# One hybrid decoder layer on one core: the 64-row products of two heads issued in turn, an own PSUM bank for the outputs of the recurrence, and two pieces of setup placed behind other work

## The chip, the core and the metric

The kernel runs on one core of one Trainium2 chip. The time of a run is that of one execution on the device, in microseconds (us). Before the change three runs gave 782.29, 787.22 and 790.95 us; the median is 787.22.

The engines in the profile are PE (TensorE's products), PEld (its weight loads), DVE (VectorE), ACT (ScalarE), POOL (GpSimd) and SP (SyncE, which issues the DMAs). A label such as L359 is a line of the kernel before; in the changed kernel the same statements stand some lines lower.

## What is computed

One decoder layer on 1024 tokens of width 1024, all in float32. A normed input is projected once; one part feeds four heads of latent attention, one part eight heads (64 wide) of a recurrence, and one part gates both.

```python
u = rmsnorm(h, norm_pre_g);  p = u @ w_in
p_mla, p_rw, z = split(p)
q, kv = ...                                  # low-rank; rope on 64 columns of q and of the key
y_mla = causal softmax attention of 4 heads  # 128 + 64 wide scores
r, k, v, xw, xa = token_shift_mix(p_rw)
decay = exp(-exp(-softplus(-(w0 + tanh(xw) @ w2)) - 0.5));  a = sigmoid(a0 + xa @ a2)
# recurrence, for each head and token:
S = S * w_t + (S @ -kk_t) (kk_t * a_t)^T + v_t k_t^T;   y_t = S @ r_t
y_rw = group_norm(y) * g + b + bonus
h = h + rmsnorm((concat(y_mla, y_rw) * silu(z)) @ w_out, norm_post_g)
```

## The kernel before

Tokens are done in two halves of 512, h = 0 and 1; inside a half the recurrence runs over 8 chunks of 64 tokens. Channels of the recurrence are four blocks of 128, and a block holds two heads: head e = 0 on partitions 0 to 63, e = 1 on 64 to 127. Two blocks make a group g, so a half has two groups of four heads.

A string `PROGRAM` lists the steps in the order in which they are recorded; a step is a letter and its indices. The whole lies in a block with a scheduler, which then places the instructions on each engine by its own model of time, so an engine's order is not that of the string: steps overlap, and products of later steps stand between those of earlier ones. Each engine then runs its list in order. Tiles with the same tag share a fixed number of buffers: in PSUM four of `pj` (projections), two of `wk`, two of `ch`, each of one bank. In SBUF `LS`, `BK`, `AB` and `SV` have two buffers each, one for each group, so the second half's units (and later the attention's tiles, which use the same tags) take them when the first half is done with them.

The steps that matter here:

- **A** (stage_a): for each of four blocks of 128 tokens of the half, the sum of squares (ACT), on POOL the two operations of `rstd` (L57, L58), on DVE the scaling (L170), on PE eight transposes (L177), and the split of the result into a high and a low part `uH` (ACT, L181) and `uL` (DVE, L182). All projections (L210) read both parts.
- **X** (op_x, lora_in): in half 0 first the low-rank weights, loaded and split on POOL (L232, L233, two of each); then one projection, shifted (L218), tanh, and the parts `xw` and `xa` that the products L250 and L251 read. Weights of a projection are split by ACT (L190) and POOL (L200, four pieces each).
- **B** (op_b): tables of sine and cosine for the rope: 25 operations on DVE (L655 to L676; L661 eight times, L667 four times) and two Sin on ACT. They are read only by the attention's steps.
- **P** (prep): projections and elementwise work for one block of 128 channels.
- **E** (units): for that block the products inside the chunks. L359: for each chunk and head a 64-row product `(64 x 128)^T (64 x 128)` into `pE[e]`, one `wk` bank for a head and four chunks; DVE reads each twice (L363, L364). L373: for each chunk and head a 64-row product with 64 columns into `pB`, one `wk` bank for a head and eight chunks, read by DVE (L374). L384 is a 128-row product and L392 four more. The masked triangles go to DRAM for the inverse.
- **I** (inverse): 62 operations on DVE (L418, L420) invert all 32 x 32 triangles, the result comes back by DMA (`sx`, `st`), then 32-row products (L447, L454) and copies into `AB` (L455, L456) finish the 64 x 64 inverses.
- **C** (chain): chunk after chunk, for both groups: R from the state (L474), copied by ACT (L476); part of the output Y (L480); the corrected values (L484), copied by ACT and DVE (L486, L487); the new state (L490), added by DVE (L494); the rest of Y (L496), copied by ACT (L499). All four results of a group lie in one `ch` bank, `pcs`:

```python
pcs = [chp((128, 4, 2, 64)) for _ in range(2)]   # 0: R, 1: Y, 2: corrected, 3: state
PE.matmul(pc[ev[e], 3, l], BK[:, l, c, e], SV[:, c, e, l], ...)      # L490
V.tensor_tensor(dst, pc[ev[e], 3], D_[ev[e]], ALU.add)               # L494
PE.matmul(pc[ev[e], 1, l], AB[ev[e], l, c, 64:128], SV[...], ...)    # L496
S.copy(SV[:, c, 0], pc[:, 1])                                        # L499
```

- **N, G**: group norm (L513) and outputs, whose transposes L525 take one head at a time, 64 rows, into a `ch` bank. **M, T**: the attention's projections (L538 to L540, 96 products a half) and their tail (L563). **Z, Y**: the gates (L210; L586 for two gates at once). **U, K, J, Q, S**: the attention and the output projection (L728, L758, L774, L794, L801, L819, L842, L863, L874, L922); some of their PSUM tiles are `wk` buffers too.

Of the kernel before, what the change touches and what calls it, by code (L numbers as in the profile page):

```python
# [44 lines left out]
def layer(tc, x, pos, w_in, w_out, w_uq, w_ukv, vecs, w2, a2, consts, post_g, out):  # L45
# [9 lines left out]
    def rstd(ss, scale):  # L55

        G.tensor_scalar(ss, ss, scale, EPS, ALU.mult, ALU.add)  # L57
        G.tensor_tensor(ss, ss, mhalf[:, 0:ss.shape[-1]], ALU.pow)  # L58
# [4 lines left out]
    with tc.tile_pool(name="sb", bufs=1) as cp, \  # L63
# [58 lines left out]
        ops.update(attention(tc, E))  # L122
        for op in " ".join(PROGRAM).split():
            name = op.rstrip("0123456789")
            ops[name](*(int(i) for i in op[len(name):]))
# [4 lines left out]
    "A0 X0 Z00 B P00 E00 Z01 P01 E01 Z02 P02 E02 P03 E03 I0 C0 N00 G00 N01 G01 M0 Z03 Z04 Z05 Y06 T0 A1 X1",  # L130
    "P10 E10 Z10 P11 E11 Z11 P12 E12 P13 E13 I1 C1 N10 G10 N11 G11 M1 Z12 T1 Z13 Z14 Z15 Z16 Z17 U K J Q0",
    "Q1 Q2 Q3 S",
)


def recurrence(tc, E):
# [13 lines left out]

    uH = alloc(P1, (128, 8, HALF), "uH", F32R)
    uL = alloc(P1, (128, 8, HALF), "uL", F32R)

    def stage_a(h):

        XT = (("v", "sq"), ("sg", "cs"), ("a", "k"), ("kf", "r"))
        for pr in range(2):
            xs = []
            for q in range(2):
# [8 lines left out]
                E["rstd"](ss[:, 0:1], 1.0 / D)  # L168
# [66 lines left out]
    def lora_in(h):  # L235
        px = shifted(proj(CO_X), V_MU_X, "v", 1)
# [8 lines left out]
        return xw, xa  # L245
# [100 lines left out]
    def units(h, cb, gt, made):  # L346
# [6 lines left out]
        for c4 in range(0, NCH, 4):  # L353
            mk = mks[c4 // 4]
            pE = [wk((128, 4, 128)) for _ in range(2)]
            for ci in range(4):
                for e in range(2):
                    r = slice(e * 64, e * 64 + 64)
                    PE.matmul(pE[e][:, ci], pl[r, c4 + ci, 1 - e:3 - e].rearrange("p a b -> p (a b)"),  # L359
                              LS[r, c4 + ci, e, :], start=True, stop=True)  # L360
# [7 lines left out]
        G.tensor_tensor(dD, bc(id2.unsqueeze(1), (128, NCH, 64)), bc(Dg.unsqueeze(2), (128, NCH, 64)), ALU.mult)  # L368
        for e in range(2):
            r = slice(e * 64, e * 64 + 64)  # L370
            pB = wk((128, NCH, 64))
            for c in range(NCH):
                PE.matmul(pB[:, c], pl[r, c, 1 - e:3 - e].rearrange("p a b -> p (a b)"), dD[r, c], start=True, stop=True)  # L373
            V.tensor_tensor(BK[:, :, e], pB, bc(rs[:, :, e:e + 1], (128, NCH, 64)), ALU.mult)  # L374
# [22 lines left out]

    ev = (slice(0, 64), slice(64, 128))
    le = [(l, e) for l in range(2) for e in range(2)]

    def inverse(h, gt):
# [37 lines left out]
        for g in range(2):  # L439
# [9 lines left out]
            for l in range(2):  # L449
# [5 lines left out]
                V.tensor_copy(AB[0:32, l, :, 32:64], pG[0:32])  # L455
                S.copy(AB[64:96, l, :, 32:64], pG[64:96])  # L456

    def chain(h, gt):

        for g in range(2):  # L460
            for e in range(2):
                G.tensor_copy(gt["g"][g]["SV"][ev[e], 0, e], Sst[ev[e], 2 * g:2 * g + 2])
        for c in range(NCH):
# [4 lines left out]
            parts = []  # L468
            for g in range(2):
                LS, BK, AB, SV = (gt["g"][g][k] for k in ("LS", "BK", "AB", "SV"))  # L470
                parts.append((LS, BK, AB, SV, Sst[:, 2 * g:2 * g + 2], gt["Dg"][:, 2 * g:2 * g + 2], pcs[g], Rs[g], SD[g]))
            for LS, BK, AB, SV, St, Dg, pc, R_, D_ in parts:
# [4 lines left out]
                for e in range(2):  # L477
                    G.tensor_tensor(D_[ev[e]], SV[ev[e], c, e], bc(Dg[ev[e], :, c:c + 1], (64, 2, 64)), ALU.mult)  # L478
                for l, e in le:
                    PE.matmul(pc[ev[e], 1, l], LS[:, l, c, e, 64:128], SV[:, c, e, l], start=False, stop=False,  # L480
                              skip_group_check=True)
            for LS, BK, AB, SV, St, Dg, pc, R_, D_ in parts:
                for l, e in le:
                    PE.matmul(pc[ev[e], 2, l], AB[ev[e], l, c, 0:64], R_[ev[e], l], start=False, stop=False,  # L484
                              skip_group_check=True)
                S.copy(SV[ev[0], c, 0], pc[ev[0], 2])  # L486
# [574 lines left out]
```

## Time and profile before

| what | before |
|---|---|
| runs: lowest, median, highest | 782.29, 787.22, 790.95 us |
| the profiled execution | 783.81 us |
| its span in the trace | 782.0 us |
| mean granted clock of TensorE | 0.951 of full |
| busy: PE, PEld, DVE, ACT, POOL | 713.0, 586.1, 466.4, 347.9, 331.9 us |
| idle TensorE: L177 waiting for its last input from DRAM at the start | 9.8 us |
| idle TensorE: L490 waiting for L487 | 4.9 us in 9 |
| idle TensorE: L177 waiting for L170 | 3.4 us in 1 |

In a row of a timeline stand the start, the duration, engine, line, operation, output and inputs, and in brackets the idle time before it with what ended it. A row may hold several instructions (`x8`); its duration then runs from the first start to the last end. A float32 product appears as two instructions. Products are pipelined: an instruction's duration is longer than the distance to the next start, so the pace is read from start to start. In the tables by stretch of time the columns are the stretch, its length, busy time and instructions of each engine, the granted clock, the share of the DMA engines and GB/s.

### The profile page before, as it was taken

To read this page: it belongs to the slowest core of one execution; us is meant where nothing else is said; L and a number is where in the kernel's file an instruction comes from. 1 tells how busy PE (TensorE), PEld (TensorE's weight loads), DVE (VectorE), ACT (ScalarE), POOL (GpSimd) and SP (SyncE) were. 2 spreads that over 40 slices of the span, in tenths; PEclk is the share of its full clock that TensorE was granted. 3 is DMA by queue.
4 is the path that set the end of the run, shared out by engine and by line. 5 is a ranking of instruction groups with operands and counts; after the bars stand their busy time and mean duration, and the time that the engine had idled before them with its cause. 6 is when DMAs were issued, how large, how long until landed. Compare 5 with 4: busy or idle time off the path is not lost. (4 is left out here: it accounts for less than half of the span.)

```text
span 782.0 us, 13855 instructions
## 1 busy us (share of the span) xinstructions
PE 713.0 (91%) x5136; PEld 586.1 (75%) x5136; DVE 466.4 (60%) x943; ACT 347.9 (44%) x877; POOL 331.9 (42%) x478
## 2 busy tenths in 40 slices
PE   2789999999978998889999989799899998899996
PEld 1667877789866776667888967577678997788885
DVE  4756757758925522495866691476497767644333
ACT  6465355343725453344353162426354566632221
POOL 6265645445942554263554374032332237442220
PEclk9999999999998899977999989879999999999999
DMA  6224241254383133043223366411023025144321
GB/s 208 80 69 115 54 114 51 68 151 134 114 187 89 28 108 83 2 89 85 57 68 97 86 171 156 131 44 42 2 55 101 21 89 162 52 166 141 121 82 54
DMA packets 118819, 72.84 MB, mean 93 GB/s; under 512 B 47072, under 2 KB 108256, under 8 KB 118752
## 3 DMA queue, kind: packets, MB, share of 16 engines
q1 hardware_dynamic: 118752, 71.96, 32.5%
q8 instruction: 40, 0.66, 0.4%
q14 instruction: 27, 0.22, 0.1%
HBM read 54.38 MB, written 17.56 MB: 92 GB/s over the span
## 5 line engine op out<-in xcount | busy, mean ns | idle before, releaser
L210 PE MATMUL pj<-uH,w 128*128 128x512 f32 x640 | 215.7, 411 | 3.3 <-DVE uL L182 2.5
L200 POOL TENSOR_TENSOR w<-wf,w 128x256 fp32r<-128x256 f32 x168 | 141.3, 871 | 116.6 <-ACT w L190 106.5
L210 PEld LDWEIGHTS pj<-uH,w 128*128 128x128 f32 x640 | 123.7, 195 | 33.1 <-DVE uL L182 2.9
L210 PE MATMUL pj<-uL,w 128*128 128x512 f32 x320 | 130.2, 407 | 0.0
L210 PEld LDWEIGHTS pj<-uL,w 128*128 128x128 f32 x320 | 62.6, 196 | 14.0 <-issue 0.8
L190 ACT CAST w<-wf 128x1024 fp32r<-128x1024 f32 (+1 forms) x50 | 51.4, 1027 | 28.8 <-PE pj L540 21.3
L478 POOL TENSOR_TENSOR SD<-SV,Dg 64x128 f32<-64x128 f32 x64 | 27.9, 436 | 74.0 <-DVE SV L494 59.9
L854 POOL TENSOR_SCALAR wf<-wf,sm 128x128 f32<-128x128 f32 (+7 forms) x32 | 24.0, 750 | 67.1 <-DVE sm L853 51.9
L198 POOL TENSOR_TENSOR w<-wf,w 128x224 fp32r<-128x224 f32 x32 | 23.8, 775 | 38.8 <-ACT w L190 32.2
L359 PEld LDWEIGHTS wk<-LS,pl 64*128 64x128 f32 x256 | 30.2, 191 | 12.5 <-issue 10.2
L979 DVE TENSOR_TENSOR LS<-pj,LS 128x512 f32<-128x512 f32 x16 | 11.1, 691 | 45.5 <-ACT cq L978 44.3
L359 PE MATMUL wk<-LS,pl 64*128 64x128 f32 x256 | 35.6, 289 | 1.3 <-DVE LS L317 1.2
L850 ACT ACTIVATE wf<-pj,mx 128x512 f32<-128x512 f32 (+3 forms) x48 | 27.7, 583 | 13.5 <-DVE mx L847 9.9
L865 ACT CAST BK<-wk 128x512 fp32r<-128x512 f32 (+3 forms) x48 | 22.4, 485 | 25.2 <-PE wk L863 23.2
L373 PEld LDWEIGHTS wk<-r,pl 64*128 64x128 f32 x256 | 29.5, 196 | 4.4 <-issue 2.9
L373 PE MATMUL wk<-r,pl 64*128 64x64 f32 x256 | 31.2, 284 | 1.2 <-DVE LS L364 1.0
L874 PE MATMUL ch<-BK,LS 128*128 128x256 f32 (+1 forms) x160 | 31.6, 282 | 0.7 <-ACT BK L865 0.7
L487 DVE COPY SV<-ch 64x128 f32<-64x128 f32 x32 | 9.2, 294 | 36.5 <-issue 25.7
L418 DVE TENSOR_TENSOR tmp<-XA 128x31 f32<-128x31 f32 (+15 forms) x62 | 28.2, 454 | 4.4 <-DMA XA<-sa 2.6
L866 DVE TENSOR_TENSOR AB<-wk,BK 128x512 fp32r<-128x512 f32 (+3 forms) x48 | 26.0, 551 | 7.3 <-ACT BK L865 6.8
L420 DVE TENSOR_TENSOR XA<-XA,tmp 128x31 f32<-128x31 f32 (+15 forms) x62 | 28.4, 458 | 1.9
L845 DVE TENSOR_REDUCE mx<-pj 128x1 f32<-128x512 f32 (+3 forms) x48 | 25.8, 551 | 6.0 <-PE pj L844 3.4
(339 smaller groups left out, 1659.4 us busy)
## 6 DMA issues: line engine op xcount, KB each, us to landing
wf<-in_w_in_dram SPq DMA_DIRECT2D x42, 512.0 KB, 3.9
zs<-st SPq DMA_DIRECT2D x16, 256.0 KB, 3.1
wf<-in_x_dram SPq DMA_DIRECT2D x8, 512.0 KB, 3.7
out_dram<-LS SPq DMA_DIRECT2D x16, 256.0 KB, 2.1
wf<-in_w_in_dram SPq DMA_DIRECT2D x8, 448.0 KB, 3.5
bvd<-st SPq DMA_DIRECT2D x8, 256.0 KB, 2.0
SV<-bvd SPq DMA_DIRECT2D x16, 128.0 KB, 3.4
yrw<-SV SPq DMA_DIRECT2D x8, 256.0 KB, 2.6
```

Of the source, the lines that this page charges most:

```text
L190: S.copy(wh, wf)
L200: G.tensor_tensor(wl[:, sl], wf[:, sl], wh[:, sl].bitcast(F32), ALU.subtract)
L210: PE.matmul(ps, w_[:, kb], u_[:, kb], start=(n == 0), stop=(n == 23))
L359: PE.matmul(pE[e][:, ci], pl[r, c4 + ci, 1 - e:3 - e].rearrange("p a b -> p (a b)"), LS[r, c4 + ci, e, :], start=True, stop=True)
L373: PE.matmul(pB[:, c], pl[r, c, 1 - e:3 - e].rearrange("p a b -> p (a b)"), dD[r, c], start=True, stop=True)
L418: V.tensor_tensor(t3, bc(At[:, j, j + 1:32].unsqueeze(2), (128, n, w)), bc(X[:, j, 0:w].unsqueeze(1), (128, n, w)), ALU.mult)
L420: V.tensor_tensor(X[:, j + 1:32, 0:w], X[:, j + 1:32, 0:w], t3, ALU.add)
L478: G.tensor_tensor(D_[ev[e]], SV[ev[e], c, e], bc(Dg[ev[e], :, c:c + 1], (64, 2, 64)), ALU.mult)
L845: V.tensor_reduce(mx[:, n5:n5 + 1], s_, axis=AX.X, op=ALU.min)
L850: S.activation(pr[:, b0:b1], sc[:, 0:b1 - b0], AF.Exp, bias=mx[:, 0:1], scale=-1.0, accum_out=sm[:, n5:n5 + 1])
L866: V.tensor_tensor(PL[:, b0:b0 + nb, o], pt[:, 0:nb], PH[:, b0:b0 + nb, o].bitcast(F32), ALU.subtract)
L874: PE.matmul(py[:, o], l_, r_, start=(j == 0 and n == 0), stop=(j == nk - 1 and n == 2), skip_group_check=True)
```

## The change

1. The rope tables (B) move in the string from half 0's X to behind A1, and a table names what two steps have to stand behind on their engines: X0's instructions behind the last `pow` of A0, B's behind the last copy of the inverse I0. The steps return those instructions for it.
2. In `units` the products of both heads are issued under an order written by hand, chunk by chunk and head by head; L373 now fills two `wk` banks together. `outputs` does the same with its transposes.
3. In `chain` the bank of a group holds three results, and Y of both groups goes to one `wk` bank of the chunk, `pY`. The products for Y are recorded behind both groups' R, and behind both groups' state; the two copies of Y stand at the end of the chunk.

```diff
-    "A0 X0 Z00 B P00 E00 ... T0 A1 X1",
+    "A0 X0 Z00 P00 E00 ... T0 A1 B X1",
+BEHIND = {"X0": "A0", "B": "I0"}
         for op in " ".join(PROGRAM).split():
             name = op.rstrip("0123456789")
-            ops[name](*(int(i) for i in op[len(name):]))
+            with tc.issue_after(done[BEHIND[op]].ins) if op in BEHIND else contextlib.nullcontext():
+                done[op] = ops[name](*(int(i) for i in op[len(name):]))
...
             pE = [wk((128, 4, 128)) for _ in range(2)]
-            for ci in range(4):
-                for e in range(2):
-                    r = slice(e * 64, e * 64 + 64)
-                    PE.matmul(pE[e][:, ci], pl[r, c4 + ci, 1 - e:3 - e].rearrange("p a b -> p (a b)"),
-                              LS[r, c4 + ci, e, :], start=True, stop=True)
+            with tc.manual_schedule(engines={PE.engine}):
+                for ci in range(4):
+                    for e in range(2):
+                        PE.matmul(pE[e][:, ci], pl[ev[e], c4 + ci, 1 - e:3 - e].rearrange("p a b -> p (a b)"),
+                                  LS[ev[e], c4 + ci, e, :], start=True, stop=True)
...
+        pB = [wk((128, NCH, 64)) for _ in range(2)]
+        with tc.manual_schedule(engines={PE.engine}):
+            for c in range(NCH):
+                for e in range(2):
+                    PE.matmul(pB[e][:, c], pl[ev[e], c, 1 - e:3 - e].rearrange("p a b -> p (a b)"), dD[ev[e], c],
+                              start=True, stop=True)
         for e in range(2):
-            r = slice(e * 64, e * 64 + 64)
-            pB = wk((128, NCH, 64))
-            for c in range(NCH):
-                PE.matmul(pB[:, c], pl[r, c, 1 - e:3 - e].rearrange("p a b -> p (a b)"), dD[r, c], start=True, stop=True)
-            V.tensor_tensor(BK[:, :, e], pB, bc(rs[:, :, e:e + 1], (128, NCH, 64)), ALU.mult)
+            V.tensor_tensor(BK[:, :, e], pB[e], bc(rs[:, :, e:e + 1], (128, NCH, 64)), ALU.mult)
...
-            pcs = [chp((128, 4, 2, 64)) for _ in range(2)]
+            pY = wk((128, 2, 2, 64))
+            pcs = [chp((128, 3, 2, 64)) for _ in range(2)]
...
+            for g, (LS, BK, AB, SV, St, Dg) in enumerate(parts):
                 for l, e in le:
-                    PE.matmul(pc[ev[e], 1, l], LS[:, l, c, e, 64:128], SV[:, c, e, l], start=False, stop=False,
+                    PE.matmul(pY[ev[e], g, l], LS[:, l, c, e, 64:128], SV[:, c, e, l], start=(g == 0 and l == 0), stop=False,
                               skip_group_check=True)
...
+            for g, (LS, BK, AB, SV, St, Dg) in enumerate(parts):
                 for l, e in le:
-                    PE.matmul(pc[ev[e], 1, l], AB[ev[e], l, c, 64:128], SV[ev[e], c, e, l], start=False,
+                    PE.matmul(pY[ev[e], g, l], AB[ev[e], l, c, 64:128], SV[ev[e], c, e, l], start=False,
                               stop=True, skip_group_check=True)
-                S.copy(SV[:, c, 0], pc[:, 1])
+            for g in range(2):
+                S.copy(parts[g][3][:, c, 0], pY[:, g])
```

What the scheduler makes of it is seen in the engines' lists. POOL near the start, where the fourth block's norm (`ss_42`) and the low-rank weights (`lora`) meet; before:

```order
L167 TENSOR_TENSOR ss_42_180<-ss_42_180 128x1
L232 TENSOR_SCALAR lora_228<-wf_229 128x512
L276 MEMSET sg_373 128x8
L57 TENSOR_SCALAR ss_42_180<-ss_42_180 128x1
L232 TENSOR_SCALAR lora_228<-wf_234 128x512
L233 TENSOR_TENSOR lora_228<-wf_229,lora_228 128x512
L58 TENSOR_TENSOR ss_42_180<-ss_42_180,mhalf_74 128x1
L233 TENSOR_TENSOR lora_228<-wf_234,lora_228 128x512
L200 TENSOR_TENSOR w_241<-wf_239,w_241 128x256 x4
```

and now (L57 and L58 are L58 and L59 here, L232 and L233 are L243 and L244, L200 is L211):

```order
L178 TENSOR_TENSOR ss_42_180<-ss_42_180 128x1
L288 MEMSET sg_334 128x8
L58 TENSOR_SCALAR ss_42_180<-ss_42_180 128x1
L59 TENSOR_TENSOR ss_42_180<-ss_42_180,mhalf_74 128x1
L243 TENSOR_SCALAR lora_228<-wf_229 128x512
L243 TENSOR_SCALAR lora_228<-wf_234 128x512
L244 TENSOR_TENSOR lora_228<-wf_229,lora_228 128x512
L244 TENSOR_TENSOR lora_228<-wf_234,lora_228 128x512
L211 TENSOR_TENSOR w_241<-wf_239,w_241 128x256 x4
```

All four splits moved behind the norm; the weight splits behind them keep their place.

On DVE at the same place the rope operations that stood between the L182 operations and ahead of the fourth block's L170 are gone; they now stand between A1's L182 operations and the first chunks' copies of the chain C0, behind the inverse I0's last copy.

PE in the first unit (E00), where `wk_106_544` and `wk_107_545` are the two heads' banks; before:

```order
L359 MATMUL wk_106_544<-LS_69_360,pl_90_431 128x128 x4
L384 MATMUL pj_113_598<-q_95_477,cst_1_64 128x512
L359 MATMUL wk_107_545<-LS_69_360,pl_90_431 128x128 x4
L210 MATMUL pj_118_620<-uH_19_98,w_117_614 128x512
L210 MATMUL pj_118_620<-uL_20_99,w_117_614 128x512
```

and now, where L359 is L372, L384 is L399 and L210 is L221, and `wk_100_505` and `wk_101_506` are the banks:

```order
L372 MATMUL wk_100_505<-LS_63_321,pl_84_392 128x128
L399 MATMUL pj_107_568<-q_89_438,cst_1_64 128x512
L221 MATMUL pj_112_590<-uH_19_98,w_111_584 128x512
...
L221 MATMUL pj_112_590<-uH_19_98,w_111_584 128x512
L372 MATMUL wk_101_506<-LS_63_321,pl_84_392 128x128
L372 MATMUL wk_100_505<-LS_63_321,pl_84_392 128x128
L372 MATMUL wk_101_506<-LS_63_321,pl_84_392 128x128
L372 MATMUL wk_100_505<-LS_63_321,pl_84_392 128x128
L372 MATMUL wk_101_506<-LS_63_321,pl_84_392 128x128
L372 MATMUL wk_100_505<-LS_63_321,pl_84_392 128x128
L372 MATMUL wk_101_506<-LS_63_321,pl_84_392 128x128
```

The first product of a block stands alone, ahead of other work, and the other seven follow in turn; L373's sixteen stand in the same way, one and then fifteen. In the last unit of half 0 (E03) 48 of the 96 products L538 to L540 now stand ahead of the second block of L359, before 19; in E13 it is nearly the same.

PE in the chain C0 where no other products stand between, from the state of one chunk to the next; before:

```order
L490 MATMUL ch_306_1991<-SV_72_363,BK_70_361 64x64 x4
L490 MATMUL ch_307_1992<-SV_76_367,BK_74_365 64x64 x4
L496 MATMUL ch_306_1991<-SV_72_363,AB_71_362 64x64 x4
L496 MATMUL ch_307_1992<-SV_76_367,AB_75_366 64x64 x4
L474 MATMUL ch_312_2053<-SV_72_363,LS_69_360 64x64 x4
```

and now (L497 is L484, L503 is L490, L509 is L496, L493 is L480, L486 is L474; `ch_313` and `ch_314` are the groups' banks, `wk_312` is pY):

```order
L497 MATMUL ch_314_2058<-Rs_316_2060,AB_69_327 64x64 x4
L509 MATMUL wk_312_2056<-SV_66_324,AB_65_323 64x64
L503 MATMUL ch_313_2057<-SV_66_324,BK_64_322 64x64 x4
L509 MATMUL wk_312_2056<-SV_66_324,AB_65_323 64x64 x3
L509 MATMUL wk_312_2056<-SV_70_328,AB_69_327 64x64
L503 MATMUL ch_314_2058<-SV_70_328,BK_68_326 64x64 x4
L509 MATMUL wk_312_2056<-SV_70_328,AB_69_327 64x64 x3
L493 MATMUL wk_319_2119<-SV_66_324,LS_63_321 64x64
L486 MATMUL ch_320_2120<-SV_66_324,LS_63_321 64x64 x4
```

The products for Y moved from behind both states to places beside them. Since `pY` holds one of the two `wk` buffers, products of the attention that use `wk` (L728, L774, and with them parts of L819 and L842) moved from the second inverse and the chain C1 to behind C1; E10's first products moved from beside C0's last chunk to behind it.

More of the change, by code (lines that the diff above doesn't have):

```diff
@@ L1 @@
+import contextlib
 import math
@@ L149, in col @@
         return vec[:, c:c + 1]
+    ev = (slice(0, 64), slice(64, 128))
+    le = [(l, e) for l in range(2) for e in range(2)]
     uH = alloc(P1, (128, 8, HALF), "uH", F32R)
     uL = alloc(P1, (128, 8, HALF), "uL", F32R)
+    last = [None]
     def stage_a(h):
@@ L483, in chain @@
                 for l, e in le:
-                    PE.matmul(pc[ev[e], 2, l], AB[ev[e], l, c, 0:64], R_[ev[e], l], start=False, stop=False,
+                    PE.matmul(pc[ev[e], 1, l], AB[ev[e], l, c, 0:64], R_[ev[e], l], start=False, stop=False,
                               skip_group_check=True)
-                S.copy(SV[ev[0], c, 0], pc[ev[0], 2])
-                V.tensor_copy(SV[ev[1], c, 1], pc[ev[1], 2])
-            for LS, BK, AB, SV, St, Dg, pc, R_, D_ in parts:
+                S.copy(SV[ev[0], c, 0], pc[ev[0], 1])
@@ L489, in chain @@
+                V.tensor_copy(SV[ev[1], c, 1], pc[ev[1], 1])
+            for (LS, BK, AB, SV, St, Dg), pc, D_ in zip(parts, pcs, SD):
                 for l, e in le:
-                    PE.matmul(pc[ev[e], 3, l], BK[:, l, c, e], SV[:, c, e, l], start=False, stop=False,
-                              skip_group_check=True)
+                    PE.matmul(pc[ev[e], 2, l], BK[:, l, c, e], SV[:, c, e, l], start=False, stop=True, skip_group_check=True)
                 for e in range(2):
                     dst = SV[ev[e], c + 1, e] if c + 1 < NCH else St[ev[e]]
-                    V.tensor_tensor(dst, pc[ev[e], 3], D_[ev[e]], ALU.add)
+                    V.tensor_tensor(dst, pc[ev[e], 2], D_[ev[e]], ALU.add)
@@ L520, in outputs @@
         SV = gt["g"][g]["SV"]
+        pT = [chp((128, NCH, 64)) for _ in range(2)]
+        with tc.manual_schedule(engines={PE.engine}):
+            for c in range(NCH):
+                for e in range(2):
+                    PE.transpose(pT[e][:, c], SV[ev[e], c, 0].rearrange("p l v -> p (l v)"), ident[ev[e], ev[e]])
         for e in range(2):
             o = SV[:, :, 1, e]
-            pT = chp((128, NCH, 64))
-            for c in range(NCH):
-                PE.transpose(pT[:, c], SV[ev[e], c, 0].rearrange("p l v -> p (l v)"), ident[ev[e], ev[e]])
-            V.scalar_tensor_tensor(o, pT, hln[:, 2 * g + e:2 * g + e + 1], o, ALU.mult, ALU.add)
+            V.scalar_tensor_tensor(o, pT[e], hln[:, 2 * g + e:2 * g + e + 1], o, ALU.mult, ALU.add)
             b = (2 * g + e) * 128
@@ L593, in recurrence, with op_a @@
     lora, xx, gts, cqs, made = {}, {}, {}, {}, {}
+    def op_a(h):
+        stage_a(h)
+        return last[0]
     def op_x(h):
@@ L597, in op_x @@
             lora_load()
[L598 removed]
+        lora_in(h)
     def op_p(h, cb):
```

27 lines of the change are left out of this document (12 added, 15 removed).

## Prediction

> **What bounds the kernel now.** I read the page's busy rows first, then a table by stage, the list of TensorE's waits, and short stretches of the timeline. The page:
>
> ```profile
> span 782.0 us, 13855 instructions
> PE 713.0 (91%) x5136; PEld 586.1 (75%) x5136; DVE 466.4 (60%) x943; ACT 347.9 (44%) x877; POOL 331.9 (42%) x478
> ```
>
> TensorE is the bound, but 91% is a mean. By stage (span in us; then each engine's busy time; then the granted clock):
>
> ```profile
> 0.00:46.00 46.00, 24.98 (x86) 19.05 (x87) 27.39 (x67) 26.16 (x51) 22.02 (x46) 0.97 0.45 130
> 46.00:180.00 134.00, 133.19 (x709) 108.12 (x708) 85.70 (x121) 60.62 (x131) 69.21 (x95) 1.00 0.34 94
> 180.00:236.00 56.00, 49.86 (x510) 43.68 (x509) 38.56 (x81) 28.83 (x73) 37.56 (x59) 0.96 0.56 145
> 236.00:330.00 94.00, 85.77 (x855) 66.34 (x855) 39.61 (x87) 41.73 (x108) 38.01 (x65) 0.92 0.21 59
> 361.00:430.00 69.00, 69.00 (x381) 56.11 (x380) 45.39 (x65) 28.49 (x65) 31.71 (x43) 1.00 0.26 71
> 430.00:500.00 70.00, 63.98 (x536) 53.01 (x534) 37.65 (x86) 25.91 (x62) 30.16 (x44) 0.93 0.50 136
> 500.00:572.00 72.00, 64.17 (x779) 50.21 (x780) 46.22 (x120) 32.23 (x118) 19.12 (x39) 0.86 0.13 40
> ```
>
> The stages of prep and units (46 to 180, 361 to 430) have no idle TensorE: there, time comes only from fewer TensorE microseconds. The start, the inverses (180 to 236, 430 to 500) and the chains (236 to 330, 500 to 572) have idle time: there a wait sets the pace. The change touches all of these; what follows 572 keeps its work.
>
> **Start.** The fourth block's norm is late:
>
> ```profile
> 14.00 0.19 POOL L57 TENSOR_SCALAR ss<-ss 128x1 f32<-128x1 f32 x1
> 14.27 0.62 POOL L232 TENSOR_SCALAR lora<-wf 128x512 fp32r<-128x512 f32 x1
> 14.85 1.27 POOL L233 TENSOR_TENSOR lora<-wf,lora 128x512 fp32r<-128x512 f32 x1
> 16.08 0.56 POOL L58 TENSOR_TENSOR ss<-ss,mhalf 128x1 f32<-128x1 f32 x1
> 17.00 3.64 DVE L661 TENSOR_SCALAR q<-cst,posf 128x32 f32<-128x32 f32 x5
> 20.56 0.48 DVE L170 TENSOR_SCALAR kf<-kf,ss 128x512 f32<-128x512 f32 x1
> 21.09 0.47 PE L177 MATMUL pj<-cst,kf 128*128 128x128 f32 x1 [3.42 <-DVE kf L170]
> 26.90 0.80 PE L210 MATMUL pj<-uH,w 128*128 128x512 f32 x1 [2.54 <-DVE uL L182]
> ```
>
> Two of the lora splits stand between L57 and L58 on POOL, five rope operations of DVE between L58's end and L170. Without both, L58 follows L57 and L170 comes some 6 us earlier, at about 14.5. After it, the last L182s lose the rope pieces between them; L667's four alone took 1.7. Against it: the splits now run together in front of the weight splits of L200, so X0's first low-part weights are no earlier than before. I take **-8** for X0's first product (26.90 to about 19); bounds -6 (the L170 shift alone) and -10.
>
> **Units.** For L359, 8 instructions are four matmuls of one head (fp32 shows as two instructions each); for L373, 32 are both heads, 16 and 16:
>
> ```profile
> 63.55 1.16 PE L359 MATMUL wk<-LS,pl 64*128 64x128 f32 x8
> 64.64 1.12 PE L384 MATMUL pj<-q,cst 128*128 128x512 f32 x2
> 78.53 3.39 PE L373 MATMUL wk<-r,pl 64*128 64x64 f32 x32
> 81.85 0.72 PE L210 MATMUL pj<-uH,w 128*128 128x512 f32 x2
> ```
>
> Start to start that is 1.09 us for eight (136 ns each) and 3.32 for 32 (104 ns). (16 blocks of L359 with 16 instructions, 8 of L373 with 32: two halves, four units, two blocks of chunks.) Can the two row halves run at once? Before, they meet where L373 goes over from the first head to the second; in the last unit of half 1 the instructions under way in three stretches of 0.40 us, and the durations (shortest, median, longest), are
>
> ```profile
> 432.90:433.30 0.40, 0.40 (x6) 1.00 0.00 0
> 433.35:433.75 0.40, 0.40 (x9) 1.00 0.91 174
> 433.75:434.15 0.40, 0.40 (x9) 1.00 0.66 215
> ```
>
> ```profile
> L373 PE MATMUL wk<-r,pl x256: 272/272/443, 78.5 to 435.2; 64*128 64x64 f32 x128
> ```
>
> Within one half 6 instructions are under way in a stretch, which (400 + 272)/104 gives; around the change of half it is 9, or one every 75 ns, in stretches that hold both kinds. So the halves overlap at least there, and I take half of the old spacing throughout: 68 ns for L359, 55 for L373 (rounded up from 52). But in the new order the first matmul of a block stands alone, ahead of other work. L359: 2 x 136 + 14 x 68 = 1.22 instead of 2.18, -0.96 in each of 16 blocks = -15.4. L373: 2 x 104 + 30 x 55 = 1.86 instead of 3.32, -1.46 in each of 8 = -11.7. Together **-27**; bounds 0 (no overlap) and -29. The trace prices the lone matmul: from a 64-row product to a 128-row one the next start comes later than between equals,
>
> ```profile
> 172.11 0.47 PE L540 MATMUL pj<-w,uL 128*128 128x448 f32 x1
> 172.42 0.36 PE L538 MATMUL pj<-w,uH 128*128 128x448 f32 x1
> 172.62 0.37 PE L539 MATMUL pj<-w,uH 128*128 128x448 f32 x1
> ```
>
> 0.31 against 0.20, so 0.1 there and as much on the way in: 24 more detours at 0.2 = **+5**, bounds 0 and +5. L525's 64 transposes, at L373's gain of 1.46/32 each, would give -3; they stand in a stretch that other waits end, so **-1**, bounds 0 and -3.
>
> The Trainium skill, "TensorE: Matmul & The Clock Gate", Part 3, Packing small matmuls, has a weight load overlap running matmuls only where the row group differs, and measured 3.07 times for four row tiles. The stretches above agree in kind. By that share of the ideal (77%) two halves would run 1.54 times as fast, and the units' gain would be an estimated 61.5 x (1 - 1/1.54) = 21 us before the detours. The Trainium skill, "TensorEngine Tiling (Array Packing)", Key Properties, also says that changing the tiling mode, and not just the tile, drains TensorE; that speaks against the lone matmuls, and the 0.1 us above is what this trace shows of it.
>
> **Before the inverses.** The scheduler placed the last unit anew: 48 instead of 19 of the M step's matmuls stand ahead of E03's second block. 29 x 0.2 = 5.9 us. The inverse begins from that block's output, and TensorE waits at its end:
>
> ```profile
> 221.09 0.31 PE L447 MATMUL ch<-XA,AB 32*32 32x32 f32 x2 [2.05 <-DMA XA<-sx]
> 481.19 0.24 PE L447 MATMUL ch<-XA,AB 32*32 32x32 f32 x2
> ```
>
> In half 0 the data come last, so the delay counts; in half 1 L447 begins without a wait, TensorE was the later one, so I count nothing. **+6**; bounds 0 and +12.
>
> **Rope tables behind I0.** About 13 us of DVE (estimate: eight of L661 at 3.64/5, L667's 1.7, thirteen more at L667's mean) now stand between the first L182s of A1 and the chain's copies; X1 waits for L182, the chain for L487 and L494, on a DVE that runs in order.
>
> ```profile
> L667 DVE SCALAR_TENSOR_TENSOR q<-q 128x256 f32<-128x256 f32 x4 | 1.7, 416 | 0.0
> 239.50 3.32 DVE L182 SCALAR_TENSOR_TENSOR uL<-pj,vec,uH 128x256 fp32r<-128x256 f32 x7 [3.11 <-ACT uH L181]
> ```
>
> DVE stood idle 3.11 just before these, and the stage uses it for 39.61 of 94; part of the 13 fills such holes. **+4**; bounds +2 and +8.
>
> **Chain.** Two bare chunks (nothing else between), 4.83 us apart:
>
> ```profile
> 555.80 0.93 PE L474 MATMUL ch<-SV,LS 128*64 128x64 f32 x16
> 556.62 0.45 PE L480 MATMUL ch<-SV,LS 128*64 128x64 f32 x8
> 557.00 0.45 PE L484 MATMUL ch<-Rs,AB 64*64 64x64 f32 x8
> 558.66 0.29 DVE L487 COPY SV<-ch 64x128 f32<-64x128 f32 x1 [0.47 <-ACT SV L486]
> 559.63 0.45 PE L496 MATMUL ch<-SV,AB 64*64 64x64 f32 x8 [0.17 <-DVE SV L494]
> 560.63 0.93 PE L474 MATMUL ch<-SV,LS 128*64 128x64 f32 x16
> ```
>
> Before, L496 waits for L494 though it needs only L487's data: bank `ch` holds both outputs. With Y in its own bank it fills the wait for the second L487, and L474 of the next chunk waits for L494 alone. A run of 8 takes 0.38 (556.62 to 557.00); a chunk has ten, so TensorE's own pace is 3.8: -1.0. That holds for bare chunks, four in each chain; the others have products between, which hide the wait. **-8**; bounds 0 and -16 (all sixteen chunks). The new bank is a `wk` buffer, one of two: rope transposes (L774) and some of L728, L819 and L842 that ran inside the second inverse and chain move behind it. Their TensorE time stays, but they no longer fill idle time: **+3**, the middle of 0 and +6 (the idle time of 430 to 500, 70.00 - 63.98, once more), since no row tells.
>
> **Sum**: -8 - 27 + 5 - 1 + 6 + 4 - 8 + 3 = -26. The profiled execution took 783.8 with its span of 782.0, 3.4 under the median of 787.2; against the median, **761**.
>
> **Rivals.**
> - *The buffers hold it up.* Both `wk` buffers are filled in turn, so a block starts only when DVE has read both of the block before: four reads, not two.
>
> ```profile
> L363 DVE TENSOR_TENSOR AB<-wk,a x16: 682/685/695, 66.3 to 423.8; 64x512 f32<-64x512 f32 x16
> DVE AB L363: 22.2, 11
> ```
>
> Two more at 0.69 = 1.4 us where a block follows closely. For it: nothing says how late DVE will be once the products come faster. Against: before, L363 waited 22.2 us for the products, so DVE is early. At half the units' gain: 774.
> - *No overlap in steady state.* The stretches at 433 might show only a weight load taken early. Units 0, the rest +1: 788.
> - *Slower: each change of half drains.* If an instruction starts only when the one before ended, 512 x 0.272 = 139 us stand where 16 x 2.18 + 8 x 3.32 = 61.5 stood: +78, **866**. It decides the sign from (61.5 + 7)/512 = 134 ns each (now 120), since the other terms sum to +1 and 1% is 8 us. Against it: the nine at 433.
> - *The change doesn't do what it says*: a turn of e = 0 and e = 1 could be undone by the scheduler; the listing of the new order shows seven of eight in turn, so only the first is lost, which is in the sum.
>
> **Numbers.** Forecast 0.62 (745 to 772 its own range), buffers 0.2, no overlap 0.12, drain 0.04, 0.02 elsewhere. The range 740 to 784 leaves out the drain, half of no overlap and a tail below. A measurement of this kernel can tell about 1%: faster by more than 1% (under 779) 0.84, within 0.1, slower 0.06.
>
> **What would show it.** L359's sixteen within about 1.3 us of TensorE and L373's thirty-two within 1.9 right; L170 of `kf` before 16 us and X0's first product near 19; bare chunks 3.8 apart; L447 of half 0 only some 20 earlier. Wrong: the alternating instructions still at 104 ns or more, idle TensorE ahead of them waiting for L363 or L374, or the chains no shorter.

## The result, and the profile after

| | before | changed |
|---|---|---|
| runs: lowest, median, highest | 782.29, 787.80, 790.95 us | 775.78, 777.38, 780.56 us |
| profiled execution, its span | 783.81, 782.0 us | 775.78, 772.4 us |
| mean granted clock | 0.951 | 0.933 |

The ratio of the changed kernel to the one before is 0.9899, 95% interval 0.9859 to 0.9939: faster by 1.0%, some 8 us by this ratio and 10 by the medians, where 26 were forecast. The page of the changed kernel (lines now: L372 was L359, L376 L363, L377 L364, L386 L373, L399 L384, L221 L210, L486 to L509 the chain's L474 to L496):

```profile
span 772.4 us, 13874 instructions
PE 689.6 (89%) x5136; PEld 564.9 (73%) x5136; DVE 454.0 (59%) x943; ACT 345.8 (45%) x875; POOL 331.1 (43%) x478
```

TensorE is busy 713.0 - 689.6 = 23.4 us less, and the span fell by 9.6: idle TensorE rose from 69.0 to 82.8. The table by stage (start; prep and units; inverse; first chain; units; inverse; second chain; the rest) shows where. Behind the start it is cut at the last L386, the first L486 and the last L506, the state's addition, of each half:

```profile
0.00:46.00 46.00, 29.64 (x123) 24.08 (x124) 20.39 (x45) 28.09 (x55) 27.38 (x51) 0.93 0.55 152
46.00:172.00 126.00, 121.99 (x709) 97.09 (x707) 77.97 (x111) 58.69 (x130) 67.47 (x97) 1.00 0.35 99
172.00:231.40 59.40, 48.09 (x504) 40.55 (x501) 39.77 (x87) 27.75 (x68) 32.36 (x53) 0.84 0.53 138
231.40:322.00 90.60, 86.04 (x844) 65.80 (x845) 45.17 (x113) 40.28 (x108) 38.41 (x63) 0.94 0.19 53
322.00:433.90 111.90, 98.01 (x599) 79.18 (x599) 69.56 (x109) 46.22 (x104) 54.51 (x73) 0.88 0.33 84
433.90:494.70 60.80, 47.77 (x458) 38.64 (x456) 38.70 (x89) 23.37 (x57) 23.27 (x34) 0.89 0.50 138
494.70:551.50 56.80, 52.80 (x727) 42.58 (x728) 39.96 (x103) 20.60 (x68) 16.64 (x36) 0.84 0.12 36
551.50:772.30 220.80, 205.24 (x1187) 177.03 (x1185) 122.53 (x293) 100.78 (x287) 71.06 (x74) 0.98 0.30 94
```

Cut at the same events, the kernel before has 131.9 and 105.6 us in the units' stages, with 0.8 and 5.4 of TensorE's idle time. Now the first has 4.0 (126.00 - 121.99) and the second, with what stands behind the first chain, 13.9; and the second is 6.3 us longer. The inverses had 58.9 and 64.9 us with 6.1 idle in each, and now have 11.3 and 13.0 idle. The products themselves did become faster. The first unit (E00) on TensorE, other products left out:

```profile
54.83 0.48 PE L372 MATMUL wk<-LS,pl 64*128 64x128 f32 x2
55.24 1.12 PE L399 MATMUL pj<-q,cst 128*128 128x512 f32 x2
...
57.69 1.16 PE L372 MATMUL wk<-LS,pl 64*128 64x128 f32 x14
58.77 0.50 PE L221 MATMUL pj<-uH,w 128*128 128x512 f32 x1
...
64.72 0.48 PE L372 MATMUL wk<-LS,pl 64*128 64x128 f32 x2
...
66.03 1.16 PE L372 MATMUL wk<-LS,pl 64*128 64x128 f32 x14
...
74.30 2.00 PE L386 MATMUL wk<-r,pl 64*128 64x64 f32 x30
76.22 0.50 PE L221 MATMUL pj<-uL,w 128*128 128x512 f32 x1
```

Start to start a block of L372 takes 0.41 + 1.08 = 1.49 us (2.18 before), and L386's thirty 1.92. And the same unit on DVE:

```profile
59.20 0.75 DVE L229 SCALAR_TENSOR_TENSOR v<-pj,vec,v 128x511 f32<-128x511 f32 x1 [3.95 <-ACT v L228]
60.43 0.69 DVE L401 TENSOR_TENSOR st<-pj,v 128x512 f32<-128x512 f32 x1 [0.48 <-ACT v L230]
61.04 0.67 DVE L376 TENSOR_TENSOR AB<-wk,a 64x512 f32<-64x512 f32 x1
61.72 0.69 DVE L377 TENSOR_TENSOR LS<-wk,cst 64x512 f32<-64x512 f32 x1
62.34 0.69 DVE L376 TENSOR_TENSOR AB<-wk,a 64x512 f32<-64x512 f32 x1
63.06 0.68 DVE L377 TENSOR_TENSOR LS<-wk,cst 64x512 f32<-64x512 f32 x1
67.02 0.68 DVE L376 TENSOR_TENSOR AB<-wk,cs 64x512 f32<-64x512 f32 x1 [3.27 <-PE wk L372]
```

Both banks are complete only at 58.8; the four reads begin at 61.04, behind `v`, and end at 63.74; the second block, which goes into the same two banks, begins at 64.72, and DVE stands idle 3.27 us for its main part. Before, the heads' banks were filled, read and filled again one behind the other:

```profile
63.55 1.16 PE L359 MATMUL wk<-LS,pl 64*128 64x128 f32 x8
...
70.88 1.16 PE L359 MATMUL wk<-LS,pl 64*128 64x128 f32 x8
```

From the first block's first product to the second's it was 7.3 us there (63.55 to 70.88) and is 9.9 now (54.83 to 64.72). TensorE does not stand still in between: it is busy in all of the 21.40 us from 54.80 to 76.20, with projections that its list has between the blocks. In the list of DVE's waits, before and after:

```profile
DVE AB L363 <- PE wk L359: 22.2, 11, 4.5
DVE BK L374 <- PE wk L373: 17.7, 4, 5.6
```

```profile
DVE AB L376 <- PE wk L372: 37.6, 8, 5.6
DVE BK L389 <- PE wk L386: 3.1, 2, 2.0
```

Together DVE waits as long for these products as before (39.9 and 40.7 us), though they run in two thirds of the time. TensorE's own waits for the reads of these banks are short, none in half 0 and 3.6 us in half 1:

```profile
PE wk L372 <- DVE LS L377: 2.3, 2, 1.4
PE wk L386 <- DVE LS L377: 1.3, 2, 0.7
```

### The profile page after: what moved, and what is told of

It reads as the page before. It is cut to its first block, busy times and chain, and to the rows that moved or that the text cites. A ratio compares the mean times of both kernels' runs of the same rounds, so it can differ in the third digit from the quotient of the medians.

```text
span 772.4 us, 13874 instructions
## 1 busy us (share of the span) xinstructions
PE 689.6 (89%) x5136; PEld 564.9 (73%) x5136; DVE 454.0 (59%) x943; ACT 345.8 (45%) x875; POOL 331.1 (43%) x478
## 4 chain that ended last, share of the span: by engine, by line
PE 36%; DVE 12%; DMA 4%; ACT 3%; POOL 2%; issue 2%; SPq 2%; DVEq 0%; ACTq 0%; POOLq 0%
PE pj L942 11%; PE pj L221 5%; PE pj L862 4%; PE ch L894 3%; DVE tmp L430 2%; PE pj L814 2%; DVE XA L432 2%; PE wk L883 2%; PE wk L372 1%; PE ch L503 1%; POOL w L211 1%; PE wk L509 1%; ACT wf L870 1%; PE pj L821 1%; DMA XA<-sa 1%
## 5 line engine op out<-in xcount | busy, mean ns | idle before, releaser
L221 PE MATMUL pj<-uH,w 128*128 128x512 f32 x640 | 214.9, 409 | 5.7 <-ACT sg L289 4.8
L211 POOL TENSOR_TENSOR w<-wf,w 128x256 fp32r<-128x256 f32 x168 | 140.0, 864 | 117.9 <-ACT w L201 106.8
L221 PEld LDWEIGHTS pj<-uH,w 128*128 128x128 f32 x640 | 121.8, 193 | 36.1 <-ACT sg L289 5.4
L221 PE MATMUL pj<-uL,w 128*128 128x512 f32 x320 | 129.4, 405 | 0.0
L221 PEld LDWEIGHTS pj<-uL,w 128*128 128x128 f32 x320 | 61.8, 193 | 14.2 <-issue 1.2
L490 POOL TENSOR_TENSOR SD<-SV,Dg 64x128 f32<-64x128 f32 x64 | 30.0, 468 | 57.2 <-DVE SV L506 47.8
L209 POOL TENSOR_TENSOR w<-wf,w 128x224 fp32r<-128x224 f32 x32 | 22.1, 722 | 25.5 <-ACT w L201 15.4
L372 PEld LDWEIGHTS wk<-LS,pl 64*128 64x128 f32 x256 | 19.3, 187 | 12.2 <-issue 11.2
L998 ACT ACTIVATE cq<-pj 128x512 bf16<-128x512 f32 x16 | 9.6, 597 | 41.1 <-PE pj L942 41.1
L894 PEld LDWEIGHTS ch<-BK,LS 128*128 128x128 f32 x160 | 26.8, 197 | 0.9 <-ACT BK L885 0.5
L513 ACT COPY SV<-wk 128x128 f32<-128x128 f32 x32 | 6.9, 269 | 45.6 <-PE wk L509 45.6
L372 PE MATMUL wk<-LS,pl 64*128 64x128 f32 x256 | 24.8, 290 | 2.7 <-DVE LS L377 2.3
```

What stands on the lines that cost most here:

```text
L211: G.tensor_tensor(wl[:, sl], wf[:, sl], wh[:, sl].bitcast(F32), ALU.subtract)
L221: PE.matmul(ps, w_[:, kb], u_[:, kb], start=(n == 0), stop=(n == 23))
L372: PE.matmul(pE[e][:, ci], pl[ev[e], c4 + ci, 1 - e:3 - e].rearrange("p a b -> p (a b)"), LS[ev[e], c4 + ci, e, :], start=True, stop=True)
L894: PE.matmul(py[:, o], l_, r_, start=(j == 0 and n == 0), stop=(j == nk - 1 and n == 2), skip_group_check=True)
```

## The experiments

Theory A: what TensorE saves turns to idle time wherever it is saved, because DVE, ACT and the DMAs pace these stages. Theory B: every part brings its forecast by itself and the parts disturb each other. Theory C, formed after the first four runs: turns make both `wk` banks of a block full at one moment, the second block waits for all four reads, and the units get their length from that and not from TensorE. Ratios are to the kernel before on the same chip, with 95% intervals.

**One part alone (three kernels).** `e1`: only the new `units` and `outputs`. `e2`: only `PROGRAM`, `BEHIND` and the returned instructions. `e3`: only the new `chain`.

> The kernel before with the products of units and the transposes of outputs in turn, and nothing else of the change. In the trace of the changed kernel a pair of halves starts 7 ns apart and pairs 105 ns apart, so TensorE needs some 19 us less for the 24 blocks. Theory A (what TensorE saves here becomes waiting: units and inverses are paced by what DVE, ACT and the DMAs do between the products): span within 4 us of the kernel before, idle TensorE up by 14 us or more. Theory B (each part brings its TensorE time when alone, and the parts spoil each other, by the shared wk buffers): 15 to 22 us faster than before.

> The kernel before with the rope tables behind the first inverse and the low-rank weights behind the first norm, and nothing else of the change. The first projection should start some 6 us earlier, as it does in the changed kernel. Theory A: those 6 us reach the end of the first units, and the tables behind the inverse give back 2 to 5 there: 1 to 5 us faster. Theory B: 4 us faster. A rival to both, that the tables in front of the first chain cost as much as the start gains: no difference (within 1 us).

> The kernel before with the own bank for Y and nothing else of the change. In the changed kernel the second chain takes 57 us instead of 74, but 13 of that come back behind it as attention work that had run inside. Theory A: bare chunks at some 4 us instead of 4.83; 4 to 9 us faster in all, so most of what the whole change gains beyond its start. Theory B: 8 to 12 us faster. A rival, that the shorter chain only moves work: no difference (within 2 us).

Measured: e1 1.0075 (1.0048 to 1.0101), slower; e2 0.9886 (0.9822 to 0.9949); e3 0.9995 (0.9963 to 1.0027). So the turns, with 20.7 us less of busy TensorE (692.3 against 713.0), cost time; the start alone brought as much as the whole change, with a wide interval; the own bank nothing. B is out: the units alone don't bring their price. A missed too: it allowed e1 4 us and gave e3 a gain of 4 to 9.

**The changed kernel without alternation.**

```diff
-                for ci in range(4):
-                    for e in range(2):
+                for e in range(2):
+                    for ci in range(4):
```

(and the same for L386 and the transposes)

> The changed kernel with the hand-written order kept, but all products of one head ahead of the other's, so that both banks are still taken together and the halves don't overlap except where the heads meet. Theory A: TensorE's time goes back up by some 19 us, and almost none of it is seen at the end: within 4 us of the changed kernel, with its idle time down by 14 or more. Theory B: 15 to 22 us slower than the changed kernel.

Measured: 0.9837 (0.9785 to 0.9889), so not slower than the changed kernel but ahead of it, by 0.6% between ratios whose intervals overlap. Its page:

```profile
span 769.6 us, 13868 instructions
PE 710.8 (92%) x5136; PEld 586.4 (76%) x5136; DVE 459.4 (60%) x943; ACT 344.0 (45%) x875; POOL 330.0 (43%) x478
```

With 21 us more of busy TensorE it ends 2.8 us earlier. That fits A, and asks what else the turns do. Without turns the blocks stand as before, and in the first unit the second follows 7.3 us behind the first (54.66 to 61.99) instead of 9.9.

**Which turns, and what stands between the blocks.** `e5`: L372 left to the scheduler, L386 and transposes in turn. `e6`: L386 as before, L372 and transposes in turn. `e7`: L372 in turn but for `cb == 3`. `e8`: `BEHIND` also holds `"M0": "E03", "M1": "E13"`, so that M's products stand behind the last unit's L386.

> The changed kernel with the products of L372 left to the scheduler (it puts one head's four behind the other's), and only those of L386 and the transposes in turn. Without any turn the kernel was 1.6% under the one before, with all of it 1.0%. Theory C (taking turns makes both wk banks of a block full at the same moment, so DVE's four reads follow instead of running beside the second head's products; a unit's first block to last block gets 2 to 3 us longer, and the last unit of each half hands that to the inverse): L386's sums are not on the inverse's path, so this is at least as fast as without any turn: 1.6 to 2.2% under the kernel before. Theory A (TensorE's saved time is idle wherever it is saved): between the two, 1.0 to 1.6% under.

> The changed kernel with L386 as before, one bank after the other, and only L372 and the transposes in turn. Theory C: as slow as the changed kernel or slower, 0.5 to 1.1% under the kernel before, the unit's first block to last block some 12 us as in the changed kernel. Theory A: between the changed kernel and the one without turns, 1.0 to 1.6% under.

> The changed kernel with L372's turns only in the first three units of each half; in the last unit, whose products the inverse waits for, they are left to the scheduler. Theory C: each inverse begins 2 to 4 us earlier than in the changed kernel, and the end moves by about as much: 1.3 to 1.9% under the kernel before. Theory A: as the changed kernel, 0.9 to 1.2% under.

> The changed kernel with the M step's products kept behind the last unit's on TensorE, in both halves (29 more of them stand ahead of the last unit's second block there than in the kernel before). TensorE then has nothing between the last unit's blocks, and waits there, but keeps 96 products for the inverse. Theory C: the inverses begin some 5 us earlier than in the changed kernel, and the end moves by most of it, twice: 1.5 to 2.3% under the kernel before. Theory A, in which the inverse's start is set by DVE and the DMAs and not by these products: as the changed kernel, 0.9 to 1.2% under.

Measured: e5 0.9869 (0.9807 to 0.9932), e6 1.0009 (0.9974 to 1.0044), e7 0.9893 (0.9845 to 0.9942), e8 1.0060 (1.0025 to 1.0095). L372's turns are the costly ones, as C says (e6 against e5), though e5 by itself lies in A's range. e7 misses C's expectation and meets A's: it moved nothing, so it isn't the last unit alone. e8 is a miss for both theories: the first inverse did begin 5 us earlier, but with none of M's products in the units TensorE stood idle 19.6 us in the second units' stage:

```profile
PE wk L372 <- DVE LS L377: 6.5, 6, 1.6
PE wk L386 <- DVE LS L377: 5.8, 6, 1.3
```

These are TensorE's waits for the banks, more than in the changed kernel, with fewer other products to cover them. The units did get shorter (the table at the end of this section), but the work came later: the first chain's L486 run from 226.0 to 315.0, where they run from 231.4 to 312.2 in the changed kernel.

**Two more banks.**

```diff
-            pE = [wk((128, 4, 128)) for _ in range(2)]
+            pE = [(wk, chp)[c4 // 4]((128, 4, 128)) for _ in range(2)]
```

`e9` has turns; `e10` has one head's products ahead of the other's, so that only those at the meeting of two blocks still go in turn. `e11` is the changed kernel with `S.copy` in place of L377, which leaves out the mask, and `e12` the changed kernel with B back in its old place.

> The changed kernel with the second block of L372 in the two ch banks, which stand empty while units run, instead of the same two wk banks. All else, the turns too, as in the changed kernel; the scheduler now puts both blocks' sixteen products together. Theory C (the two wk banks, full at one moment, make the second block wait for DVE's four reads of the first, which stand behind other DVE work): first to last product of L372 from some 12 us to under 4, the inverses begin 5 us or more earlier, and the end follows: 2.0 to 3.5% under the kernel before. Theory A (the stage is paced by DVE and ACT work whatever the banks): no better than the kernel without turns, 1.2 to 1.7% under.

> The kernel of the run before this with one head's products ahead of the other's, as in the run without alternation. What the turns alone are worth where no bank is waited for. Theory C: 0.5 to 1.5% slower than with turns. Theory A: the same within 0.4%, since TensorE's time is not what sets the pace.

> The changed kernel with the second read of each bank of L372 (L377) done by ACT as a plain copy, which leaves out its triangular mask; DVE reads each bank once. Theory C: the banks come free up to 1.4 us earlier in each of 16 blocks: 1.3 to 2.0% under the kernel before. Theory A, in which DVE's amount of work sets the pace: 32 reads of 0.69 us fewer on DVE, also 1.3% or more under. A rival to both, that waits come from DVE's order and not from its work: as the changed kernel, 0.8 to 1.2% under.

> The changed kernel with the rope tables back behind the first gate at the start; the low-rank weights stay behind the first norm. It prices the tables' two places. The forecast gave 4 us for the new place, and at the start the tables' five operations stand ahead of the fourth block's scaling for 3.6 us: the first projection 3 to 5 us later than in the changed kernel, the first chain's end as much earlier relative to its start, so 0.6 to 1.2% under the kernel before, about as the changed kernel. If the new place is free instead: 0.3 to 0.6% under.

Measured: e9 0.9768 (0.9705 to 0.9830), e10 0.9993 (0.9951 to 1.0034), e11 0.9854 (0.9803 to 0.9906), e12 0.9873 (0.9805 to 0.9942). With two more banks the turns are worth 2.2%. A, which allowed 0.4%, is out; C has the sign, but forecast 0.5 to 1.5%. e11, with half of the bank reads off DVE, is not told apart from the changed kernel, and its interval overlaps the ranges of A, of C and of the rival. e12 is not told apart either: the tables' new place shows no gain there, so what of the start reaches the end would have come with the low-rank weights.

**The same, with the one disturbed place mended.** In the first unit of half 1 the `ch` banks are still the first chain's: there the second block keeps `wk`. `e13` is the changed kernel with this line:

```diff
+            pE = [(chp if c4 and (h, cb) != (1, 0) else wk)((128, 4, 128)) for _ in range(2)]
```

`e14` is e13 without turns, as e10 is e9 without them, `e15` is e9 with the old chain, `e16` is e13 with B in its old place, `e17` the kernel before with nothing but the turns and these banks, `e18` is e13 with the old chain.

> The kernel with four banks and turns, but in the first unit of half 1, where the ch banks are taken by the first chain and its transposes, the second block goes back to the wk banks (with ch banks it ended 19 us after the changed kernel's there). Theory C (banks pace the units): this wait goes, and the end comes 2 to 6 us earlier than with four banks everywhere: 2.5 to 3.1% under the kernel before. A rival, that DVE's work behind the first chain (its norm) paces that place whatever the banks: as with four banks everywhere, 2.1 to 2.5% under.

> The kernel of the run before this one without turns. It repeats, with the disturbed place mended, the question what turns are worth where no bank is awaited. With four banks everywhere that was 2.2%. Theory C: 1.2 to 2.4% slower than with turns. If the first answer came from that one place: within 0.6% of it.

> Four banks everywhere and turns, with the chain of the kernel before (no own bank for Y). What the own bank is worth when the units are no longer held up. The own bank alone gave nothing; in the changed kernel's trace the second chain is 17 us shorter and 13 come back behind it. If the own bank brings its bare chunks' 8 us: 1.2 to 1.6% under the kernel before. If it only moves work: 2.0 to 2.5% under, as with it.

> Four banks but for the first unit of half 1, turns, own bank, and the rope tables back at the start. In the changed kernel the tables' place made no difference. If that holds here: as without this, 2.4 to 3.0% under. If their place behind the inverse only cost nothing there because the first chain's start waited for something else, it comes out 0.4% or more to the better here, at 2.9 to 3.5% under.

> The kernel before with the turns (as in the first run) and, as the only other edit, the second block in the ch banks but for the first unit of half 1. The forecast's term for the units, by itself: 27 less 5 for the detours, 22 us. Theory C: 2.0 to 3.0% under the kernel before, where turns alone were 0.75% over. If much of the gain of the four banks needs the earlier start or the own bank: 0 to 1% under.

> Four banks but for the first unit of half 1, turns, early start and late tables, and the chain of the kernel before. What the own bank is worth in the fastest version (3.5% under with it). If it brings its bare chunks' time there: 2.2 to 2.8% under without it. If it only moves work, as with four banks everywhere: 3.2 to 3.7% under.

| kernel | median us | ratio, 95% interval |
|---|---|---|
| e13: changed, four banks | 759.0 | 0.9649, 0.9606 to 0.9692 |
| e14: e13 without turns | 780.4 | 0.9934, 0.9894 to 0.9974 |
| e15: four banks everywhere, old chain | 767.45 | 0.9772, 0.9718 to 0.9825 |
| e16: e13, tables first | 764.13 | 0.9715, 0.9664 to 0.9767 |
| e17: before, turns and four banks alone | 760.32 | 0.9686, 0.9616 to 0.9756 |
| e18: e13, old chain | 755.6 | 0.9635, 0.9580 to 0.9689 |

The turns are worth 2.9% where the banks are free (e13 against e14), and with the two more banks alone bring 3.1% over the kernel before (e17). Both, and e13 itself, lie somewhat above C's ranges, so C's sizes were too small. The own bank is worth nothing in either version. The fastest is e18, ahead of both kernels. The first unit of e13, products and reads:

```profile
55.21 0.71 PE L372 MATMUL ch<-LS,pl 64*128 64x128 f32 x8
55.86 1.12 PE L399 MATMUL pj<-q,cst 128*128 128x512 f32 x2
61.05 0.43 PE L386 MATMUL wk<-r,pl 64*128 64x64 f32 x2
```

```profile
58.95 0.68 DVE L376 TENSOR_TENSOR AB<-wk,a 64x512 f32<-64x512 f32 x1
...
63.61 0.68 DVE L377 TENSOR_TENSOR LS<-ch,cst 64x512 f32<-64x512 f32 x1
```

Both blocks are done by 55.9, the eight reads run in one string from 58.95 to 64.3, and L386 begins at 61.05, as the two `wk` banks are read: 7.3 us behind the unit's first product (53.77), where it was 18.2 in the changed kernel (54.83 to 73.04). In e13's list of DVE's waits no row of L376 for L372 is left, only 1.1 us for ACT's mask:

```profile
DVE AB L376 <- ACT cs L352: 1.1, 1, 1.1
```

**By stage.** The traces show by which way this reaches the end, and where it is lost. In each half "units" runs from the first projection (half 0) or the first L372 (half 1) to the last L386, "inverse" from there to the chain's first product; "M" is how many of the half's 96 products of the M step stand on TensorE ahead of that last L386. Times in us, from one profiled execution each.

| kernel | units 0 | M | inverse 0 | units 1 | M | inverse 1 |
|---|---|---|---|---|---|---|
| before | 151.0 | 31 | 59.0 | 110.5 | 31 | 64.9 |
| e4: two banks, no turns | 150.5 | 31 | 64.1 | 110.6 | 50 | 60.4 |
| changed: two banks, turns | 151.0 | 78 | 59.4 | 118.4 | 78 | 60.8 |
| e8: changed, M behind | 144.7 | 0 | 61.2 | 108.7 | 0 | 70.1 |
| e14: four banks, no turns | 140.5 | 6 | 75.1 | 100.5 | 6 | 68.5 |
| e13: four banks, turns | 135.0 | 17 | 66.8 | 98.9 | 17 | 66.8 |

With two banks the turns shorten no unit's stage. Against the kernel before they save 8 x 0.69 + 4 x 1.0 = 9.5 us of TensorE's time in each half, but 47 more of M's products stand there, at 0.2 us each 9.4 us, and idle time rises by 3.0 and 8.5 us. With four banks, by an edit of nothing else, 17 stand there and not 78, and the units are 16.0 and 19.5 us shorter. So the banks act through the list: with two of them taken in turn, other products stand between the blocks, and TensorE hardly waits for a bank; where M's products are kept out (e8), it does. That the scheduler places them so because it counts the banks as taken fits this, but is not shown.

The units of e14 are shorter than e4's by 10.0 and 10.1 us without turns, yet e14 is the slower kernel: its inverses are 11.0 and 8.1 us longer. In half 0 the last block of L372 ends 9 us earlier than in e4, but the inverse on DVE begins only 1.7 earlier, behind a longer wait for its triangles from DRAM (e4, then e14):

```profile
171.99 0.19 DVE L430 TENSOR_TENSOR tmp<-XA 128x31 f32<-128x31 f32 x1 [1.75 <-DMA XA<-sa]
```

```profile
170.32 0.19 DVE L430 TENSOR_TENSOR tmp<-XA 128x31 f32<-128x31 f32 x1 [6.65 <-DMA XA<-sa]
```

From e14 to e13 the units give 5.5 and 1.6 us, and the first inverse, which holds no turns, 8.3. So the 2.9% between them is the turns with the placement that came of them; the turns' own share is not shown apart.

## Why the prediction was wrong, point by point

- **Start**, -8: the first L221 came at 20.95 instead of 26.90, -6, the near bound. The mechanism was right (POOL's `pow` directly behind; the fourth block's scaling at 15.02 instead of 20.56), and about half of it is the tables' (with them at the old place, in e12, the first projection is only 2.8 earlier). At the end e2 shows 1.1%, 9 us where start and tables together were forecast at 4, and e18 against e17 about half a per cent.
- **Units**, -27 and +5: right as TensorE's time. The blocks measured 1.49 and 2.3 us against the forecast's 1.42 and 2.06 with the detour, 16 x 0.69 + 8 x 1.0 = 19 us against 22. (The 136 and 104 ns were means over whole runs. In the kernel before, instructions within one half start every 112 ns in L359 and in L373; the 136 takes in some 0.2 us on the way in and on the way out, the 104 the place where the heads meet.) **Here the prediction failed**, at its first step: "there, time comes only from fewer TensorE microseconds" was read as "each of them brings time", with the list of products as it stood. None reached the end (e1, e4): in each half the 9.5 us saved were filled by 47 more of M's products, 9.4 us, and by new idle time. e17, with turns and two more banks, gains 24.5 us by the medians, but that is the two together and no proof of the 22. The rival "the buffers hold it up" named the cause, but priced it at half the units' gain; it took all of it. Its way was not quite the one named: the second block follows 9.9 us behind the first instead of 7.3 by its place in the list, while TensorE waits for these reads 3.6 us in all. So "L363 waited 22.2 us, so DVE is early" was right as a reading, and no argument against the rival.
- **Before the inverses**, +6: right that M's products moved ahead, but too small: 47 in each half stand ahead of the last L386, where 29 in one half were priced and nothing in the other (29 x 0.2 is 5.8, not 5.9). In half 0 the first L447, forecast some 20 us earlier, came 6.3 earlier (221.09 to 214.75). Keeping M's products behind the units (e8) shortens these, but makes the kernel slower, since they come back in the stages behind.
- **Tables**, +4: not seen. Their old place is not told apart from the new one in the changed kernel (e12) and, in the faster version, 0.7% worse (e16).
- **Chain**, -8 and +3: the pace was right and the sum wrong. A bare chunk in the changed kernel takes 3.9 us (forecast 3.8):

```profile
307.56 0.27 PE L486 MATMUL ch<-SV,LS 128*64 128x64 f32 x1
...
311.45 0.27 PE L486 MATMUL ch<-SV,LS 128*64 128x64 f32 x1
```

  The second chain, from its first L486 to its last addition of the state, is 17 us shorter (74.0 to 56.8), but the stretch from its end to the output projection 13 longer (109.8 to 122.8), because the attention's first products now stand behind it. Alone, with four banks everywhere and in the fastest version the bank is worth nothing (e3, e15, e18): the moved work should have been priced at nearly all of the gain, not at 3.
- "No overlap" and "drain" are refuted by the blocks' times; that the change doesn't do what it says, by the listing and the 23.4 us.

That the measured 777 us lies near the buffers rival's 774 is in part luck: the rival kept half of the units' gain, of which nothing came, and the start brought more than its price.

What stays open: four banks without turns (e10, e14) are slower than two banks without turns (e4) by their inverses, but only the later start of the work on DVE is seen there, not all of the 11 us. The scheduler places the whole list anew in each version, so a ratio between two of them holds its placement too; no run keeps the placement and changes the banks alone, and the kernel before with four banks and no turns was not run.

## What to carry to other kernels

A product that gets faster brings time only if its buffer comes free faster too: before counting an engine's saved microseconds, follow one buffer round its loop (filled, read, filled again) and ask what the new order does to each leg. Here, work on two banks in turn needed two more to go on with. Where a scheduler places the list anew, count what now stands in the stage before pricing what the change saves in it: a buffer that is short can show as other work in between, and not as a wait.

## What was not expected of the hardware

Turns of two 64-row halves run at the same pace whether an instruction has 64 or 128 columns. Instructions under way in 0.40 us, in a block of L372 (128 columns) and one of L386 (64):

```profile
58.00:58.40 0.40, 0.40 (x12) 1.00 0.00 0
```

```profile
74.80:75.20 0.40, 0.40 (x12) 1.00 0.00 0
```

(400 + 272)/12 is one every 56 ns; the single starts are 7 and 105 ns apart in turn. So the two halves overlap fully: 56 is half of the 112 ns within one half. Those are the same for both widths too; in the kernel before, six instructions of L359 are under way in such a stretch, as in L373's that the prediction shows:

```profile
64.00:64.40 0.40, 0.40 (x6) 1.00 0.13 22
```

And a pause of under 2.5 us can halve the granted clock, but its length alone does not tell whether it does. The changed kernel waits 2.39 us at 34.61, and the stretch behind it runs at 0.50; after the 2.27 us that end at 124.25 it stays at 1.00; in e7 the same wait, 2.28 us at the same place, is followed by a drop (0.59 is the mean of the stretch, part of it at 0.50). The rows are those of the changed kernel, and then of e7:

```profile
34.61 0.76 PE L262 MATMUL pj<-xw,lora 128*128 128x512 f32 x1 [2.39 <-DVE xw L254]
124.25 0.50 PE L221 MATMUL pj<-uH,w 128*128 128x512 f32 x1 [2.27 <-ACT sg L289]
```

```profile
34.60:37.80 3.20, 3.19 (x8) 0.50 0.65 177
38.00:41.00 3.00, 3.00 (x14) 1.00 0.66 175
...
124.30:127.60 3.30, 3.30 (x15) 1.00 0.21 80
```

```profile
124.32 0.51 PE L221 MATMUL pj<-uH,w 128*128 128x512 f32 x1 [2.28 <-ACT sg L289]
```

```profile
124.30:127.60 3.30, 3.28 (x9) 0.59 0.21 79
```

The mean clock fell from 0.951 to 0.933 with the longer idle time of the changed kernel. That its waits made the products beside them slower fits this; what it cost at the end is not shown.
